# Opening, row factor and HGRN scores of a two-layer hybrid decoder trunk: two load queues, later squares, one compact score tile

## The chip, the cores and the metric

One core of one Trainium2 chip runs the whole program in one launch. The metric is the device time of one execution in microseconds (us); lower is better. The kernel before takes 960.01 us in the median of 3 executions (957.48 to 962.03).

## The reference, cut to what matters

Two layers, each a parallel mixer and a gated MLP, on x of 256 tokens by 1024 features, float32:

```python
for l in range(2):
    xn = rmsnorm(h, norm_mix_g[l])            # h * rsqrt(mean(h*h) + eps) * g
    z = xn @ w_in[l]                          # [RWKV-7 896 | attention 1152 | mLSTM 1032 | HGRN2 1024 | gates 4096]
    y = [rwkv7(zA), dilated_attention(zB), mlstm(zC), hgrn2(zD)]
    h = h + (sum(sigmoid(gate_b) * (y_b @ P_b) for b in 4)) @ w_out[l]
    xn = rmsnorm(h, norm_ffn_g[l])
    h = h + conv_ffn(xn)                      # up 1024 -> 2 x 2816, conv of width 3, silu gate, down
return rmsnorm(h, final_norm_g)

def hgrn2_chunk(q, k, v, logf):               # chunks of 64 tokens, 4 heads of 64 channels
    decay[t, s, c] = exp(b[t, c] - b[s, c])   # s <= t, b = cumsum(logf)
    attn[t, s] = sum_c q[t, c] * k[s, c] * decay[t, s, c]
    o = (q * exp(b)) @ S + attn @ v
```

The row factor of a norm, rsqrt(mean(h*h) + eps), is one number per token. It can therefore be applied to the columns of xn before a product, or to the product's result.

## The kernel before, in words

**Activations and weights.** The residual hT lies transposed in SBUF: 8 blocks of 128 features by 256 tokens. Every product with a weight is made in three matmuls (`mm3`, lines 343 to 345) of two-part numbers: hi times hi, lo times hi and hi times lo, where hi is the value rounded to fp32r and lo is the rest. Weights come as 314 tiles of up to 128x1024 in the order of `plan()`: DMA to `raw` (3 buffers), `hi` by a cast on ScalarE (ACT, line 298), `lo` by a subtraction on VectorE (DVE, line 299), 4 buffers each. A "column group" (`ct_group`) is 256 output features from two weight tiles: 2 x 8 x 3 = 48 matmuls of 128x256. `tok_group` gives tokens in the partitions.

**The norm.** `norm_block` makes X["u"] (xh, xl): h times g, without the row factor. `sum_block` squares the blocks and adds them up in `acc`, `row_factor` sums over features on TensorE (PE; psr) and takes the power -0.5 on GpSimd (POOL, `rc`), `row_bcast` spreads it by a matmul (psb) and an ACT copy to R. The first groups of a norm use X["u"] and are multiplied by R when they leave PSUM (`evac` for rw0 to rw3, line 591; `zf`, line 1393, for the up groups j < JU = 4). Meanwhile X["s"] (sh, sl), scaled by R, is made block by block: sh on ACT, sl on POOL (line 438). The groups that follow use it: HGRN's q and f (hgq, hgf), then hgt (v and g), and in the MLP up group 4.

**The opening.** SyncE's queue (SP) sends all loads: halves of weight tiles 0 and 1 between the quarters of x (hT), then the parameters pr, tile 2, rowt, lort, and at tile 3 the constants (ident, cft, cit). 16 warm-up matmuls run on PE. ACT works off xh, the squares and the casts in turn.

**Background work.** rwkv(), hgrn(), attn() and mlstm() are generators. `step()` advances them between matmuls of the column groups; the framework's scheduler then fixes each engine's order when the program is built, and each engine works strictly in that order.

**HGRN scores.** hgrn() has products of the forget gate in Pf (tile thf) and Q, doubles the segment length h from 1 to 128, and for each h makes scaled keys kt and queries qs (qsb, two buffers, line 1004 and 1007), a score product on PE (`pdl`) and a merge into the score tile A. A holds 8 blocks of 128x128; for h up to 32 the merge is four `copy_predicated` of 64x128 each (line 1069), for each token half pj and head parity par, since the two halves lie on A's two diagonal 64x64 blocks. The diagonal (`pdg`) is put in by four products with ident. For h = 64 and 128 ACT copies. Then `po` multiplies A with V.

Of the kernel before, what the change touches and what calls it, by code (L numbers as in the profile page):

```python
# [18 lines left out]
T = 256  # L19
# [10 lines left out]
WARM = 16  # L30
# [189 lines left out]
def trunk(tc, x, wst, prm, rows, lora, fing, cfd, cid, out, dbg=None, depth=DEPTH):  # L220
# [20 lines left out]
    nc.scalar.dma_start(pr0, prm[0][:, PC["gmix"][0]:PC["gmix"][0] + 8])  # L241
# [25 lines left out]
    dummy = cp.tile([128, 1], F32, name="dummy")  # L267
# [18 lines left out]
    def w_dma(i, part=None):  # L286
# [3 lines left out]
        nc.sync.dma_start(raws[i][:, q], wst[i, :, q])  # L290

    def w_split(i, parts=1):
        r = raws.pop(i)
        hi = wp.tile([128, GW], F32R, name=f"hi{i}", tag="hi", bufs=4)
        lo = wp.tile([128, GW], F32R, name=f"lo{i}", tag="lo", bufs=4)
        for q in range(parts):
# [3 lines left out]
        his[i] = (hi, lo)  # L300
# [3 lines left out]
    def w_ahead(n):  # L304
        while ws["dma"] < min(n, NG):
            if ws["dma"] == 6:
                late_consts()
            w_dma(ws["dma"])
            ws["dma"] += 1
# [92 lines left out]
    def sum_block(m):  # L402
        if m < 2:
            ac.activation(acc[:, m, :], hT[:, m, :], AF.Square)
        else:
            sq = sqp.tile([128, T], F32, name="sq")
            ac.activation(sq, hT[:, m, :], AF.Square)
# [48 lines left out]
    w_dma(0, 0)  # L456
    x_dma(0)
    x_dma(1)
    w_dma(0, 1)
# [11 lines left out]
    norm_block(0, pr0[:, 0:1])  # L471
    w_split(0, 2)
    for m in range(1, 8):
        norm_block(m, pr0[:, m:m + 1])
    w_split(1, 2)
    ws["split"] = 2


    for l in range(depth):
        with ExitStack() as lx:  # L480
# [3 lines left out]
            (nc.sync if l == 0 else nc.gpsimd).dma_start(pr, prm[l])  # L484
            if l == 0:
                w_ahead(5)
# [5 lines left out]
            with ExitStack() as mxs:  # L492
# [4 lines left out]
                (nc.sync if l == 0 else nc.gpsimd).dma_start(rowt, rows[l])  # L497
                lort = mp("lort", bufs=1).tile([128, 256], F32, name="lort")
                (nc.sync if l == 0 else nc.gpsimd).dma_start(lort, lora[l])
# [12 lines left out]
                ve.tensor_scalar(hb_ng, P("hng", 0, 2), 0.5, None, op0=OP.mult)  # L512
                ve.tensor_scalar(hb_bg, P("bg", 0, 32), 0.5, None, op0=OP.mult)
                ve.tensor_scalar(hpar[:, 32:36], P("w0", 0, 4), 0.5, None, op0=OP.mult)
                ve.tensor_scalar(c_ka, P("ka", 0, 2), -1.0, 1.0, op0=OP.mult, op1=OP.add)
                ve.tensor_scalar(c_mu, P("mu", 0, 7), -1.0, 1.0, op0=OP.mult, op1=OP.add)
# [69 lines left out]
                def rw_cols():  # L586
                    nonlocal R

                    def evac(g, ps):
                        for cs_, p_ in ps:  # L590
                            ve.tensor_tensor(zr[:, 2 * g:2 * g + 2, 1:][:, cs_], p_, bc2(R, cs_.stop - cs_.start), op=OP.mult)

                    def scale(ms):
                        for m in ms:
                            if m % 2 == 0:
                                tmp = gtp.tile([128, 2, T], F32, name="xsc", tag="gt")
                            scaled_block(m, P("gmix", m), R, tmp[:, m % 2, :])

                    u = X["u"]
                    if l == 0:  # L600
                        for m in range(8):
                            sum_block(m)
                    ps0 = ct_group("rw0", outer=(l > 0), a=u)
                    rc = row_factor(f"m{l}")
# [11 lines left out]
                    evac(2, ct_group("rw2", a=u))  # L616
# [322 lines left out]
                def hgrn(zz, sp):  # L939
# [20 lines left out]
                    thf = sp.tile([128, 2, T], F32, name="thf")  # L960
# [6 lines left out]
                    Q = sp.tile([128, 2, T], F32, name="Q")  # L967
                    gp.memset(Q, 1.0)
                    yield
# [67 lines left out]
                    while h <= 128:  # L1037
# [27 lines left out]
                        if h <= 32:  # L1065
                            for pj in range(2):
                                r = slice(pj * 64, pj * 64 + 64)
                                for par in range(2):
                                    ve.copy_predicated(A8[r, par * 4:par * 4 + 4, r].rearrange("p e (s w h) -> p e s w h", w=2, h=h)[:, :, :, 1, :],
                                                       hgm(i)[r].rearrange("p (s h) -> p s h", h=h)[:, None].to_broadcast([64, 4, 32 // h, h]),  # L1070
                                                       pds[0][r, :, par, :].rearrange("p e (s h) -> p e s h", h=h))
# [230 lines left out]
                rw_cols()  # L1302
                grw = rwkv()
# [61 lines left out]
            with ExitStack() as fxs:  # L1365
# [7 lines left out]
                JU = 4  # L1373
# [145 lines left out]
```

## Time and profile before

| | us |
|---|---|
| median of 3 executions (957.48 to 962.03) | 960.01 |
| the profiled execution, its own time | 969.59 |
| its span, first to last instruction | 967.0 |
| PE busy in the span | 936.8 |
| VectorE busy | 741.9 |
| ScalarE busy | 560.9 |
| GpSimd busy | 231.8 |

PE is busy in 97% of the span, so the time is what PE has to do, plus its waits, plus the stretches in which its clock was granted at half. The profile gives the waits by the line that waited and the engine that ended the wait, and by window the busy time and the granted clock (1.00 is 2.4 GHz, 0.50 is 1.2 GHz). A layer is its mixer, then its MLP.

### The profile page before, as it was taken

What the parts mean: (1) busy time and instruction counts of PE and PEld (TensorE: products, weight loads), DVE (VectorE), ACT (ScalarE), POOL (GpSimd) and SP (SyncE); (2) the same over time, 40 slices, a digit from 0 to 9 for tenths busy, and PEclk for the clock granted to TensorE, in tenths of its full rate; (3) what the DMA queues carried; (4) which work ended last, traced back from release to release, by engine and by line L of the source; (5) the groups of instructions that cost most, each with busy time, mean ns of one, the idle gap of its engine ahead of it and who ended that gap; (6) DMA issues with size and microseconds to landing.
All of it is one profiled execution on the core that took longest, in us unless ns stands there. A gap on an engine that the chain in (4) does not pass through costs nothing. (4 is left out here: it accounts for less than half of the span.)

```text
span 967.0 us, 21817 instructions
## 1 busy us (share of the span) xinstructions
PE 936.8 (97%) x8884; PEld 882.9 (91%) x8884; DVE 741.9 (77%) x1180; ACT 560.9 (58%) x953; POOL 231.8 (24%) x228
## 2 busy tenths in 40 slices
PE   7999999999999999999999999999999999999996
PEld 5988998989999999999998989888989999999885
DVE  6899775669688998876688996745878889888643
ACT  6874455565556676664478634454745657766533
POOL 3500220114308621120142004101223473111102
PEclk8999999999999999999999999999999999999998
DMA  7644353434466465556555344453445646656551
GB/s 251 197 152 145 109 165 119 148 121 161 142 197 196 153 211 183 196 172 195 186 179 177 124 128 144 133 150 123 149 137 186 202 142 215 204 192 192 186 194 66
DMA packets 48980, 160.09 MB, mean 166 GB/s; under 512 B 5872, under 2 KB 7408, under 8 KB 48752
## 3 DMA queue, kind: packets, MB, share of 16 engines
q1 hardware_dynamic: 46944, 155.55, 49.7%
q10 hardware_dynamic: 1584, 2.10, 0.8%
q8 instruction: 69, 1.13, 0.5%
q0 software_dynamic: 352, 1.06, 0.4%
q14 instruction: 31, 0.25, 0.1%
HBM read 156.06 MB, written 1.05 MB: 162 GB/s over the span
## 5 line engine op out<-in xcount | busy, mean ns | idle before, releaser
L299 DVE TENSOR_TENSOR lo<-raw,hi 128x1024 fp32r<-128x1024 f32 (+4 forms) x314 | 379.2, 1212 | 150.7 <-ACT hi L298 149.5
L298 ACT CAST hi<-raw 128x1024 fp32r<-128x1024 f32 (+4 forms) x314 | 308.1, 984 | 292.8 <-PE gate L344 77.5
L344 PE MATMUL up<-sl,hi 128*128 128x256 f32 x576 | 161.7, 281 | 3.3 <-POOL sl L438 3.1
L345 PE MATMUL up<-sh,lo 128*128 128x256 f32 x576 | 161.3, 280 | 0.0
L343 PE MATMUL up<-sh,hi 128*128 128x256 f32 x576 | 161.2, 280 | 0.0
L343 PE MATMUL gate<-sh,hi 128*128 128x256 f32 x512 | 146.8, 287 | 0.0
L345 PE MATMUL gate<-sh,lo 128*128 128x256 f32 x512 | 144.6, 282 | 0.0
L344 PE MATMUL gate<-sl,hi 128*128 128x256 f32 x512 | 143.1, 279 | 0.0
L344 PEld LDWEIGHTS up<-sl,hi 128*128 128x128 f32 x576 | 108.9, 189 | 4.3 <-POOL sl L438 4.3
L343 PEld LDWEIGHTS up<-sh,hi 128*128 128x128 f32 x576 | 110.0, 191 | 0.0
L345 PEld LDWEIGHTS up<-sh,lo 128*128 128x128 f32 x576 | 108.8, 189 | 0.0
L343 PEld LDWEIGHTS gate<-sh,hi 128*128 128x128 f32 x512 | 96.8, 189 | 3.8 <-issue 0.8
L345 PEld LDWEIGHTS gate<-sh,lo 128*128 128x128 f32 x512 | 96.9, 189 | 1.8 <-issue 0.8
L344 PEld LDWEIGHTS gate<-sl,hi 128*128 128x128 f32 x512 | 96.9, 189 | 0.6 <-issue 0.3
L1421 POOL TENSOR_TENSOR af<-sf,cvf 128x256 f32<-128x256 f32 x44 | 42.8, 974 | 165.2 <-ACT sf L1419 165.2
L1417 DVE SCALAR_TENSOR_TENSOR cvf<-up,pr,cvf 128x255 f32<-128x255 f32 (+1 forms) x144 | 68.9, 479 | 2.6
L553 POOL TENSOR_TENSOR merged<-merged,gt 128x512 f32<-128x512 f32 x16 | 34.4, 2152 | 88.8 <-DVE gt L551 86.2
L344 PE MATMUL dn<-alo,hi 128*128 128x256 f32 x176 | 49.4, 281 | 0.0
L345 PE MATMUL dn<-ahi,lo 128*128 128x256 f32 x176 | 49.4, 281 | 0.0
L343 PE MATMUL dn<-ahi,hi 128*128 128x256 f32 x176 | 49.3, 281 | 0.0
L1414 ACT ACTIVATE cvf<-up,pr 128x256 f32<-128x256 f32 x72 | 40.3, 560 | 1.6 <-DVE cvf L1417 1.6
L438 POOL TENSOR_TENSOR sl<-xsc,sh 128x256 fp32r<-128x256 f32 x32 | 39.2, 1258 | 0.0
(458 smaller groups left out, 2334.1 us busy)
## 6 DMA issues: line engine op xcount, KB each, us to landing
raw<-in_wst_dram SPq DMA_DIRECT2D x254, 512.0 KB, 3.8
raw<-in_wst_dram SPq DMA_DIRECT2D x28, 256.0 KB, 2.9
raw<-in_wst_dram SPq DMA_DIRECT2D x16, 448.0 KB, 3.1
raw<-in_wst_dram SPq DMA_DIRECT2D x8, 392.0 KB, 3.6
zrot<-zrot ACTq DMA_DIRECT2D x24, 64.0 KB, 3.0
cft<-in_cf_dram SPq DMA_DIRECT2D x1, 1041.0 KB, 6.6
hT<-in_x_dram SPq DMA_DIRECT2D x4, 256.0 KB, 6.1
raw<-in_wst_dram SPq DMA_DIRECT2D x8, 128.0 KB, 2.3
```

The costliest lines, as they stand in the source:

```text
L298: ac.copy(hi[:, c], r[:, c])
L299: ve.tensor_tensor(lo[:, c], r[:, c], hi[:, c].bitcast(F32), op=OP.subtract)
L343: te.matmul(o, lh, rh, start=first, stop=False)
L344: te.matmul(o, lh, rl, start=False, stop=False)
L345: te.matmul(o, ll, rh, start=False, stop=last)
L438: gp.tensor_tensor(lo[:, m, :], tmp, h[:, m, :].bitcast(F32), op=OP.subtract)
L553: gp.tensor_tensor(mo, mo, g, op=OP.add)
L1414: ac.activation(cv[:, n, :], z[:, n, :], AF.Identity, bias=P("fcb", cj), scale=P("fcw", 88 + cj))
L1417: ve.scalar_tensor_tensor(cv[:, n, d:], z[:, n, 0:T - d], P("fcw", 44 * i + cj), cv[:, n, d:], op0=OP.mult, op1=OP.add)
L1421: gp.tensor_tensor(a_, s, cv[:, 0, :], op=OP.mult)
```

## The change

- **Opening.** Tile 0 is sent by ACT's queue and the quarters of x by SP's, behind pr0. Tile 0 is split in quarters between the norm blocks. ident, pr, rowt, lort, cit and cft go between later tiles. 12 warm-up matmuls instead of 16. In layer 0 the squares wait on purpose (their scale `late1` is a one that is computed from the end of tile 1's hi) and stand behind rw0; the row factor is taken after rw1, and R in the middle of rw2, so that rw0, rw1 and rw2 are all in PSUM before R.
- **Row factor at evacuation.** hgq (both layers) and hgf (layer 0) use X["u"] and are multiplied by R on DVE; before, both used X["s"] and were copied by ACT. JU is 5 instead of 4.
- **HGRN scores.** Scores of both token halves stand in one compact tile Ad of 128 partitions by 4x2x64. The merge for h up to 32 is one `copy_predicated` of 128x256, the diagonal two products with idm (made on POOL). A takes the memory of Pf and Q (one tile PQ), so at h = 64 POOL clears its lower left part and ACT copies Ad onto its diagonal, after the last use of Pf and Q.

```diff
-    nc.scalar.dma_start(pr0, prm[0][:, PC["gmix"][0]:PC["gmix"][0] + 8])
+    between = {4: [lambda: nc.sync.dma_start(ident_t, cfd[:, 0:128])],
+               8: [lambda: nc.sync.dma_start(cit, cid)],
+               9: [lambda: nc.sync.dma_start(cft, cfd[:, 128:])]}
...
-    w_dma(0, 0)
+    nc.sync.dma_start(pr0, prm[0][:, PC["gmix"][0]:PC["gmix"][0] + 8])
+    w_dma(0, 0, nc.scalar)
     x_dma(0)
     x_dma(1)
-    w_dma(0, 1)
+    w_dma(0, 1, nc.scalar)
...
-    norm_block(0, pr0[:, 0:1])
-    w_split(0, 2)
-    for m in range(1, 8):
-        norm_block(m, pr0[:, m:m + 1])
+    norms((0, 1))
+    w_split(0, 4, (0, 1))
+    norms((2, 3, 4, 5))
+    w_split(0, 4, (2, 3))
+    norms((6, 7))
     w_split(1, 2)
+    ve.tensor_tensor(late1, his[1][0][:, GW - 1:GW].bitcast(F32), his[1][0][:, GW - 1:GW].bitcast(F32), op=OP.is_equal)
...
-                    ps1 = ct_group("rw1", a=u, mid=get_R)
+                    if l:
+                        get_rc()
+                        ps1 = ct_group("rw1", a=u, mid=get_R)
+                        ps2 = None
+                    else:
+                        ps1 = ct_group("rw1", a=u, mid=lambda: [sum_block(m, late1) for m in range(8)])
+                        get_rc()
+                        ps2 = ct_group("rw2", a=u, mid=get_R)
...
-                        ps = ct_group("hg" + nm)[0][1]
+                        direct = l == 0 or i == 0
+                        ps = ct_group("hg" + nm, **({"a": X["u"]} if direct else {}))[0][1]
-                        ac.copy(z, ps)
+                        if direct:
+                            ve.tensor_tensor(z, ps, bc2(R, 2), op=OP.mult)
+                        else:
+                            ac.copy(z, ps)
...
-                        for pj in range(2):
-                            r = slice(pj * 64, pj * 64 + 64)
-                            ve.tensor_tensor(A8[r, par * 4:par * 4 + 4, r], pds[par][r], ident[r, r][:, None, :].to_broadcast([64, 4, 64]), op=OP.mult)
+                        ve.tensor_tensor(Ad[:, :, par, :], pds[par], idm[:, None, :].to_broadcast([128, 4, 64]), op=OP.mult)
...
+                        if h == 64:
+                            gp.memset(A8[64:128, :, 0:64], 0.0)
+                            for pj in range(2):
+                                r = slice(pj * 64, pj * 64 + 64)
+                                ac.copy(A8[r].rearrange("p (a e) t -> p e a t", a=2)[:, :, :, r], Ad[r])
-                        if h <= 32:
-                            for pj in range(2):
-                                r = slice(pj * 64, pj * 64 + 64)
-                                for par in range(2):
-                                    ve.copy_predicated(A8[r, par * 4:par * 4 + 4, r].rearrange("p e (s w h) -> p e s w h", w=2, h=h)[:, :, :, 1, :],
+                        if h <= 32:
+                            ve.copy_predicated(Ad.rearrange("p e a t -> p (e a) t").rearrange("p e (s w h) -> p e s w h", w=2, h=h)[:, :, :, 1, :],
...
-                JU = 4
+                JU = 5
```

**What moves.** First ACT's order from tile 3's cast (raw_153 before, raw_190 after) and what stands around it in the opening; sq are the squares, lw the low-rank weights' two parts, hi tile casts, hpar a small parameter. Before:

```order
L298 CAST hi_224<-raw_151 128x1024
L407 ACTIVATE sq<-hT 128x256
L946 ACTIVATE hpar<-hpar 128x4
L407 ACTIVATE sq<-hT 128x256
L642 CAST lw<-lort 32x256 x4
L642 CAST lw<-lort 64x256 x2
L298 CAST hi_228<-raw_153 128x1024
L298 CAST hi_262<-raw_155 128x1024
L429 COPY Rm_330<-psbm_327 128x256
```

And after, from tile 2's cast (raw_188) to tile 5's (raw_195):

```order
L299 CAST hi_197<-raw_188 128x1024
L404 ACTIVATE acc<-hT,dummy 128x256 x2
L407 ACTIVATE sq<-hT,dummy 128x256 x2
L970 ACTIVATE hpar<-hpar 128x4
L299 CAST hi_201<-raw_190 128x1024
L407 ACTIVATE sq<-hT,dummy 128x256
L662 CAST lw<-lort 32x256 x4
L662 CAST lw<-lort 64x256 x2
L407 ACTIVATE sq<-hT,dummy 128x256 x3
L299 CAST hi_232<-raw_193 128x1024
L299 CAST hi_265<-raw_195 128x1024
```

All eight squares now stand between tile 2's and tile 4's cast, with the six lw casts ahead of the last three; before, six of them stood ahead of tile 2's. Tile 4 is the first of rw2.

Second, DVE in layer 0's HGRN stage, around one level of the doubling. Before, the level h = 16:

```order
L767 TENSOR_TENSOR LR<-pl,cft 128x512 x2
L1015 TENSOR_TENSOR Q<-Q,thf 128x8x32
L1069 COPY_PREDICATED A<-cit,pdl 64x4x2x16 x4
L792 COPY_PREDICATED TT<-cit,LR 32x256 x4
L1016 TENSOR_TENSOR thf<-thf 128x8x32
L998 TENSOR_TENSOR thq<-zhf,Q 128x4x64
```

After, the merges of h = 1 and 2, from the queries (qsb) of h = 4 to those of h = 8:

```order
L1034 TENSOR_TENSOR qsb_900<-zhq,PQ 64x8x32 x2
L1045 TENSOR_TENSOR PQ<-PQ 128x64x4
L1100 COPY_PREDICATED Ad<-cit,pdl 128x256
L300 TENSOR_TENSOR lo_1032<-raw_881,hi_1031 128x1024
L1046 TENSOR_TENSOR PQ<-PQ 128x64x4
L1028 TENSOR_TENSOR kt_840<-zhf,PQ 128x32x8
L1100 COPY_PREDICATED Ad<-cit,pdl 128x128x2
L1034 TENSOR_TENSOR qsb_901<-zhq,PQ 64x8x32 x2
```

The merge is one instruction per level. PE's order moves with it: before, 159 matmuls of column groups stand between the score products of h = 4 and h = 128 in layer 0, after 92; and the first `po` stands behind 584 of these matmuls of the layer before, behind 511 after. In layer 1 the score products of h = 4 to 128 span 166 before and 92 to 98 after.

## Rows read from the trace of the kernel before

**Rows 1.** The page: span, and each engine's busy us, share, instructions.
```profile
span 967.0 us, 21817 instructions
PE 936.8 (97%) x8884; PEld 882.9 (91%) x8884; DVE 741.9 (77%) x1180; ACT 560.9 (58%) x953; POOL 231.8 (24%) x228
```
**Rows 2.** PE's waits over the whole span: total us, times, longest.
```profile
PE up L344 <- POOL sl L438: 3.1, 3, 1.7
PE pdl L1045 <- DVE qsb L1004: 3.0, 3, 1.9
...
PE hgq L344 <- POOL sl L438: 2.3, 3, 1.0
...
PE psbm L426 <- POOL rcm L419: 1.6, 1, 1.6
```
**Rows 3.** Windows, layer 0: us; PE, PEld, DVE, ACT, POOL busy; PEclk, DMA share, GB/s.
```profile
6.40:13.02 6.62, 3.93 (x24) 3.08 (x23) 5.46 (x15) 6.58 (x17) 3.01 (x4) 0.91 1.05 394
13.02:18.65 5.63, 5.63 (x26) 5.63 (x27) 5.45 (x17) 4.60 (x11) 0.29 (x1) 0.50 0.97 360
...
24.01:48.62 24.61, 23.32 (x198) 22.84 (x199) 21.93 (x28) 20.16 (x39) 14.26 (x12) 1.00 0.61 196
...
84.31:86.92 2.61, 0.68 (x16) 0.48 (x16) 2.51 (x8) 1.78 (x3) 0.00 (x0) 1.00 0.54 185
86.92:90.33 3.41, 3.41 (x24) 3.29 (x21) 3.38 (x7) 0.00 (x0) 0.00 (x0) 0.50 0.41 153
90.33:110.00 19.67, 19.43 (x216) 18.29 (x215) 18.79 (x41) 8.68 (x15) 0.73 (x1) 1.00 0.42 126
```
**Rows 4.** ACT in the opening, in order of time: start, us, what [idle before].
```profile
3.84 0.62 ACT L298 CAST hi<-raw 128x512 fp32r<-128x512 f32 x1 [1.17 <-DMA raw<-in_wst_dram]
5.25 0.91 ACT L399 ACTIVATE xh<-hT,pr 128x256 fp32r<-128x256 f32 x2 [0.79 <-DMA hT<-in_x_dram]
...
12.40 1.03 ACT L298 CAST hi<-raw 128x1024 fp32r<-128x1024 f32 x1
...
14.05 0.40 ACT L407 ACTIVATE sq<-hT 128x256 f32<-128x256 f32 x1
14.36 2.51 ACT L642 CAST lw<-lort 32x256 fp32r<-32x256 f32 x6
```
**Rows 5.** DVE from 48.62 to 110 us by shape: count, busy us, mean ns.
```profile
L299 DVE TENSOR_TENSOR lo<-raw,hi 128x1024 fp32r<-128x1024 f32 x16 | 19.5, 1221 | 0.5 <-ACT hi L298 0.5
L1069 DVE COPY_PREDICATED A<-cit,pdl 64x128 f32<-64x128 int32 x24 | 7.0, 352 | 0.3
...
L1033 DVE TENSOR_TENSOR A<-pdg,ident_t 64x256 f32<-64x256 f32 x4 | 1.7, 420 | 0.1
```
**Rows 6.** DVE from 110 to 128 us: another merge from PSUM.
```profile
L809 DVE COPY_PREDICATED T__1430<-cit,pd 128x256 f32<-128x256 int32 x2 | 0.9, 452 | 1.1 <-PE pd L808 1.1
```
**Rows 7.** ACT from 100 to 112 us: copies from PSUM.
```profile
L775 ACT COPY bkT<-pb 128x512 f32<-128x512 f32 x2 | 1.1, 594 | 0.0
...
L1075 ACT COPY A<-pdl 64x256 f32<-64x256 f32 x2 | 0.6, 367 | 0.6 <-PE pdl L1056 0.6
```
**Rows 8.** Windows of both MLPs' starts and of layer 1's mixer, columns as in rows 3.
```profile
307.00:328.00 21.00, 19.80 (x164) 19.18 (x164) 17.36 (x21) 11.61 (x23) 18.84 (x18) 1.00 0.52 169
...
487.80:522.50 34.70, 33.34 (x279) 32.65 (x278) 29.70 (x57) 28.14 (x53) 16.55 (x18) 1.00 0.54 181
...
549.00:580.00 31.00, 29.09 (x307) 27.05 (x307) 30.30 (x68) 13.49 (x23) 0.86 (x2) 1.00 0.38 120
...
796.00:800.30 4.30, 2.21 (x17) 1.81 (x16) 3.25 (x4) 0.97 (x3) 4.30 (x4) 1.00 0.77 243
800.30:803.72 3.42, 3.42 (x18) 3.42 (x18) 3.42 (x6) 3.42 (x7) 1.83 (x3) 0.50 0.72 183
```
**Rows 9.** Windows of PE alone in both MLPs: us, busy, matmuls, clock, DMA.
```profile
340.00:424.00 84.00, 84.00 (x716) 1.00 0.60 193
...
830.00:897.00 67.00, 67.00 (x594) 1.00 0.60 193
```

More of the change, by code (lines that the diff above doesn't have):

```diff
@@ L266, in trunk @@
     ve.memset(ones, 1.0)
-    dummy = cp.tile([128, 1], F32, name="dummy")
+    dummy_t = cp.tile([128, 2], F32, name="dummy")
+    dummy, late1 = dummy_t[:, 0:1], dummy_t[:, 1:2]
     nhalf = cp.tile([128, 8], F32, name="nhalf")
@@ L284, in trunk, with w_dma @@
     raws, his = {}, {}
-    def w_dma(i, part=None):
+    def w_dma(i, part=None, eng=nc.sync):
         if not part:
@@ L289, in w_dma, with w_split @@
         q = slice(0, sizes[i]) if part is None else slice(sizes[i] // 2 * part, sizes[i] // 2 * (part + 1))
[L290 to L296, printed above, removed]
+        eng.dma_start(raws[i][:, q], wst[i, :, q])
+    def w_split(i, parts=1, some=None):
+        r = raws[i]
+        if i not in his:
+            his[i] = (wp.tile([128, GW], F32R, name=f"hi{i}", tag="hi", bufs=4),
+                      wp.tile([128, GW], F32R, name=f"lo{i}", tag="lo", bufs=4))
+        hi, lo = his[i]
+        for q in some or range(parts):
             c = slice(sizes[i] * q // parts, sizes[i] * (q + 1) // parts)
@@ L305, in w_ahead @@
         while ws["dma"] < min(n, NG):
-            if ws["dma"] == 6:
-                late_consts()
+            for send in between.pop(ws["dma"], ()):
+                send()
             w_dma(ws["dma"])
@@ L400, in norm_block, with sum_block @@
         ve.scalar_tensor_tensor(lo[:, m, :], hT[:, m, :], gcol, h[:, m, :].bitcast(F32), op0=OP.mult, op1=OP.subtract)
-    def sum_block(m):
+    def sum_block(m, one=1.0):
         if m < 2:
-            ac.activation(acc[:, m, :], hT[:, m, :], AF.Square)
+            ac.activation(acc[:, m, :], hT[:, m, :], AF.Square, scale=one)
         else:
             sq = sqp.tile([128, T], F32, name="sq")
-            ac.activation(sq, hT[:, m, :], AF.Square)
+            ac.activation(sq, hT[:, m, :], AF.Square, scale=one)
             (ve if m >= 6 else gp).tensor_tensor(acc[:, m % 2, :], acc[:, m % 2, :], sq, op=OP.add)
@@ L496, in trunk @@
                 rowt = mp("rowt", bufs=1).tile([128, 512], F32, name="rowt")
-                (nc.sync if l == 0 else nc.gpsimd).dma_start(rowt, rows[l])
                 lort = mp("lort", bufs=1).tile([128, 256], F32, name="lort")
-                (nc.sync if l == 0 else nc.gpsimd).dma_start(lort, lora[l])
+                if l:
+                    nc.gpsimd.dma_start(rowt, rows[l])
+                    nc.gpsimd.dma_start(lort, lora[l])
+                else:
+                    between[7] = [lambda: nc.sync.dma_start(rowt, rows[0]), lambda: nc.sync.dma_start(lort, lora[0])]
                 hpar = mp("hpar", bufs=1).tile([128, 66], F32, name="hpar")
@@ L596, in scale, with get_rc @@
                                 tmp = gtp.tile([128, 2, T], F32, name="xsc", tag="gt")
-                            scaled_block(m, P("gmix", m), R, tmp[:, m % 2, :])
+                            scaled_block(m, P("gmix", m) if l else pr0[:, m:m + 1], R, tmp[:, m % 2, :])
                     u = X["u"]
-                    if l == 0:
-                        for m in range(8):
-                            sum_block(m)
                     ps0 = ct_group("rw0", outer=(l > 0), a=u)
-                    rc = row_factor(f"m{l}")
+                    rc = None
+                    def get_rc():
+                        nonlocal rc
+                        rc = row_factor(f"m{l}")
                     def get_R():
@@ L615, in rw_cols @@
                     scale(range(4, 8))
-                    evac(2, ct_group("rw2", a=u))
+                    evac(2, ps2 or ct_group("rw2", a=u))
                     hi, lo = w_next()
@@ L959, in hgrn @@
                     ve.tensor_scalar(lbnH, lbA, -0.5, None, op0=OP.mult)
-                    thf = sp.tile([128, 2, T], F32, name="thf")
+                    PQ = sp.tile([128, 2, 2, T], F32, name="PQ")
+                    thf = PQ[:, 0]
                     thq = sp.tile([128, 2, T], F32, name="thq")
@@ L966, in hgrn @@
                     gp.memset(kt1, 0.0)
-                    Q = sp.tile([128, 2, T], F32, name="Q")
+                    Q = PQ[:, 1]
                     gp.memset(Q, 1.0)
+                    idm = sp.tile([128, 64], F32, name="idm")
+                    lm2 = C("lmask")
+                    gp.tensor_tensor(idm, lm2[:, 64:128], lm2[:, 0:64], op=OP.subtract)
                     yield
```

39 lines of the change are left out of this document (20 added, 19 removed).

## The prediction

> **What bounds the kernel now.** The page's head comes first: PE is busy for 936.8 of 967.0 us [rows 1]. The change takes away none of PE's weight products, so it can gain only what PE waits, what it does at half clock, and the four warm-up matmuls. The table of PE's waits names the places [rows 2]: MLP groups that wait for POOL's sl (3.1 us), HGRN's score products that wait for the queries on DVE (3.0), hgq that waits for sl (2.3), and the spread of the row factor that waits for POOL (1.6). Then the windows show what such a wait costs beyond itself. In layer 0's opening PE is busy for 3.93 of 6.62 us, and the next 5.63 us are granted at 0.50: 26 matmuls take 0.217 each there, against 0.113 at full clock (67.0 us for 594) [rows 3, 9]. The same happens after the score wait at 84.31 (next 3.41 us at 0.50) [rows 3] and in layer 1's MLP (busy 2.21 of 4.30 us, next 3.42 us at 0.50) [rows 8]. So the clock fell to 1.2 GHz behind each of these waits, and such a wait is paid about twice. I make the sum against the profiled execution, 969.6 us, and carry the difference to the median, 960.0.
>
> **Opening (term 1).** DMA share is 1.05 at 394 GB/s from 6.40 to 13.02 us [rows 3], with one queue. I therefore let the second queue bring nothing: the two halves of tile 0 and the four quarters of x, 1.5 MB, land as now, only in another order. Were the second queue's rate added on top, tile 0's 0.5 MB would cost x nothing, 1.3 us at that rate, and the first matmuls would end by so much sooner. The Trainium skill (page "DMA: Bandwidth & Descriptors", section "Issuing engines are not separate DMA queues") speaks against that: transfers that several engines issue run on the same 16 DMA engines and interleave, and only issue time is saved. By this rule the split's own share is 0, as in my sum; the busy share above agrees.
>
> What gains is the order on ACT and DVE. The first data came at 3.84 (tile 0) and 5.25 (x) [rows 4]; sharing the engines, I let both be there at 5.2. ACT then does two quarter casts (0.35 each, estimated from half casts of 0.62), two xh (0.91), the early xsc (0.45, as an xh), two quarter casts, six xh (0.45 each): 10.7 [rows 4]. DVE's xl is 0.42 behind (its price for 256 columns [rows 5]), so weight tile 0's 24 matmuls end at 11.5. Tile 1's two casts end at 11.9, its lo parts (about 0.65 each, half of a whole tile's 1.22) let the next 24 matmuls run from 12.1 to 14.8, at full clock. Before, these 48 ended at 18.65, the end of the half-clock window. Tile 2: cast 1.03, lo 1.22 [rows 4, 5], the lo behind six small operations on pr, for which I allow 0.9: 14.7, no wait; its 24 matmuls end at 17.5, against 18.65 + 24 x 0.117 = 21.5 before. That is 4 us.
>
> Then ACT falls behind. From 12.9 it has four squares (1.6), the small exponential that sits behind DVE's lo (to 15.1), tile 3's cast (1.03), a square, the six lw casts (2.51), three squares (1.2) and only then tile 4's cast: 21.2, its lo at 22.4 [rows 4]. PE is through rw1 (24 more matmuls) at 20.2, so it waits 2.2 us in front of rw2: the new wait in the place of the 1.6 for the row factor and of hgq's share. The other 168 matmuls up to hgt are 19.0 us, the small products of the norm and of the low-rank part 1.6, and I allow 1.0 for the latter, whose inputs now come from a DVE that has the hgq evacuation (about 0.6, as ACT's copy of that size [rows 7]) on top: 22.4 + 19.0 + 1.6 + 1.0 = 44.0. Before, hgt begins at 48.62, the end of a window [rows 3]. **Gain 4.6.** Bounds: 7.8 if both new waits are hidden; 2.0 if the half clock comes as before (26 matmuls x 0.104 = 2.7).
>
> **HGRN scores (term 2).** Layer 0: 24 merges, 7.0 us busy, become 6 of 0.45 (nearest row: a 128x256 merge from PSUM, 452 ns [rows 6]), and four diagonal products of 0.42 become two: 5.2 us less on DVE, which is busy 18.79 of 19.67 us from 90.33 to 110 [rows 3, 5]. PE's loss there is 2.61 - 0.68 = 1.9, plus 1.7 for the half clock, plus 19.67 - 19.43 = 0.2 from 90.33 on: 3.8 [rows 3], the most that can come back. But PE's order is tightened too: between the scores of h = 4 and h = 128 stand 92 matmuls instead of 159. PE needs 92 x 0.113 + 2.5 for score products + 1.8 for pl + some 2 for changes between them, 16.7. DVE has in that stretch five lo (1.2 each), some 16 products (0.34 each where they overlap, an estimate from 0.42), three pairs of queries (0.85), six merges and two score masks (0.6), 17.9 [rows 5, 6]. So PE waits about 1.0 again. At the end a chain is added: POOL clears (I allow 0.2 past the copies' own wait), ACT copies Ad to A twice (0.59 each) and the h = 64 scores twice (0.37 [rows 7]), 2.1 us, in front of `po`, behind which PE stands after some 10 matmuls (1.1): another 1.0. **Gain 3.8 - 2.0 = 1.8**, bounds 3.8 and -1.5 (the half clock comes again, at either place). Layer 1: PE waits 1.9 in 549 to 580 [rows 8]. There only 6 matmuls stand between the last scores and `po`, so the copy chain shows 1.4, the DVE 0.5 to 1: **gain 0**, bounds 1.9 and -2.
>
> **hgq on X["u"], layer 1 (term 3).** From 487.8 to 522.5 PE loses 1.36 us [rows 8], nearly all hgq's wait for sl. hgf is 48 matmuls, 5.5 us, later, when sl is there. The evacuation moves from ACT to DVE, which is busy 29.7 of 34.7 us there; it stays hidden while the lo tiles are ahead. **Gain 1.3**, bounds 1.4 and 0.
>
> **JU = 5 (term 4).** Layer 0: 21.0 - 19.8 = 1.2 us of wait; layer 1: 4.30 - 2.21 = 2.1, and 1.7 of the 3.42 at half clock [rows 8]. Group 5 starts 5.5 us after group 4, and POOL is through before. Cost: one more evacuation per layer, about 0.6 on DVE, which is busy 17.36 of 21.0 us in layer 0's start; the tiles of hi and lo that stand ready (4 buffers) hide it, and without them it would stand on the path. **Gain 1.2 + 3.8 = 5.0**, bounds 5.0 and 2.5.
>
> **Sum:** 4.6 + 1.8 + 0 + 1.3 + 5.0 = 12.7. Profiled 969.6 becomes 956.9, the median 960.0 becomes 947.3; I say **947**. Bounds of all terms: 940 and 959.
>
> **Rivals.**
> (a) All waits go and none come: 7.8 + 3.8 + 1.9 + 1.4 + 5.0 = 19.9, so 940. For it: DVE loses 10 us of work in two layers. Against: ACT's order above, in which nothing is shorter, and the tightened PE order.
> (b) The opening's clock still falls: by the sum above PE idles some 1.5 us between the first and the second quarter of x, and 4 fewer warm-up matmuls precede it. Term 1 is 2.0, the time 950. For it: the drop before came with 3.93 of 6.62 us busy. Against: slower matmuls fill the 2.2 us that PE would otherwise wait for tile 4.
> (c) The scores are placed too early: DVE falls behind at each level, the clock falls in both layers. Terms 2 are -1.5 and -2: 953. It decides where a wait in front of pdl or po becomes as long as the 1.9 us at 84.31.
> (d) Slower: the pace of PE's products. With the same code, clock and tile sizes the up groups take 84.0/716 = 0.117 us per matmul in layer 0 and 67.0/594 = 0.113 in layer 1 [rows 9]. 314 tiles make up to 7500 such matmuls, 30 us between all at the one and all at the other pace, and layer 0's 1056 up matmuls are at the slow one. If shifted waits put 5000 more there, 20 us are lost and the time is 967. It decides from about 3200 on, where the 12.7 are used up. For it: the pace is set by something other than clock or shape. Against: nothing in the change aims at it, and it can as well go to the fast side, 937.
> (e) The edits do not reach the path, since waits return elsewhere (the merge into `wo`, the MLP's lo tiles): within 0.5%, some 957.
>
> **How the numbers follow.** 0.5% of 960 is 4.8 us, about what a measurement of this kernel can tell from no change. Forecast (943 to 951) 0.55; (a) with the fast side of (d) 0.13; (b) 0.12; (c) 0.09; (e) 0.06; (d) slow 0.05. The range 937 to 956 takes in (a), (b) and (c) and leaves out half of (e), (d) and the lower end, under 2 in 10. Faster by over 0.5% (below 955.2): 0.55 + 0.13 + 0.12 + 0.07 = 0.87. Same: 0.02 + 0.06 + 0.01 = 0.09. Slower: 0.04.
>
> **What would show it.** Opening: hgt's first matmul near 44 us, no half-clock window before 20 us, a PE wait of about 2 us in front of rw2 behind ACT's hi or DVE's acc and lo. HGRN: six merges per layer near 0.45 us, DVE still over 90% busy, short waits of pdl and one of po for ACT's copies, full clock at 80 to 95 us. hgq and up without waits for sl; no half clock in layer 1's MLP. The prediction would be wrong if the waits for pdl and po grow past 4 us, if a half-clock window returns in three places, or if the share of slow-paced matmuls changes by thousands.

## The result

The changed kernel takes 957.07 us (median of 20 runs, 952.51 to 963.77), the kernel before 962.40 beside it (20 runs, 957.48 to 969.83): a ratio of 0.9935, interval 0.991 to 0.996. It is faster, by 5.3 us in the medians and 6.3 by the ratio where 12.7 were forecast, and it lies 1.1 us above the range. The forecast started from 960.01, the median of three executions; 20 of them give 962.40, so 2.4 us of the miss against 947 are in that start, and the rest is in the gain.

The two profiled executions differ by more (969.59 and 956.87, spans 967.0 and 955.1), by chance exactly the 12.7 of the forecast. Nearly half of that isn't the change, which only the runs below show. Each of PE's products runs at one of two paces, and in the profile of before the slow one held through most of layer 0's up and down products, in that of after it did not: some 1,170 slow products fewer, 5.3 us at 4.5 ns each. The page of after, against [rows 1]:

```profile
span 955.1 us, 21775 instructions
PE 929.6 (97%) x8880; PEld 876.0 (92%) x8880; DVE 730.2 (76%) x1148; ACT 564.3 (59%) x956; POOL 237.6 (25%) x230
```

PE's waits from 6 to 955 us of after, against [rows 2] (total us, times, longest):

```profile
PE rw L343 <- DVE zr L602: 3.7, 2, 1.9
PE pp L343 <- ACT yhC L584: 2.7, 2, 1.4
PE pdl L1073 <- DVE Ad L1061: 2.3, 1, 2.3
PE psrm L416 <- DVE acc L410: 1.3, 1, 1.3
PE psw L691 <- DVE la L663: 1.1, 1, 1.1
PE psrf L416 <- DVE acc L410: 1.1, 1, 1.1
PE pdl L1073 <- DVE qsb L1034: 0.8, 2, 0.4
PE pdl L1087 <- DVE qsb L1037: 0.6, 1, 0.6
```

The waits for POOL's sl are gone, as the change intends, and so is POOL's rcm in layer 0 (the row factor's input, 1.6 us before). New ones stand in their place: rw3 in both layers for zr, the evacuation of the first group (1.7 and 1.9), psrm for the sum of squares, psw for la. pdl still waits: 3.7 in all, against 3.9 before (3.0 of it in [rows 2], the rest in two smaller rows).

The opening of after by windows, columns as in [rows 3]:

```profile
6.83:20.32 13.49, 12.82 (x96) 11.90 (x96) 12.51 (x36) 12.30 (x29) 4.09 (x6) 1.00 1.01 397
20.32:23.73 3.41, 1.73 (x13) 1.46 (x13) 3.03 (x6) 3.28 (x4) 0.99 (x2) 1.00 0.04 14
23.73:27.14 3.41, 3.41 (x19) 3.41 (x18) 1.57 (x2) 0.45 (x1) 1.00 (x1) 0.50 0.87 245
27.14:35.75 8.61, 6.87 (x59) 6.66 (x59) 6.45 (x8) 6.20 (x14) 4.91 (x6) 1.00 0.61 209
35.75:47.95 12.20, 11.09 (x98) 10.93 (x97) 12.01 (x17) 10.24 (x21) 7.58 (x7) 1.00 0.39 130
```

Up to 20.3 us the forecast holds to 0.2 us: 96 products in place of the half-clock window of before. Then three things come in a row. PE stands; the DMA share is 0.04, so nothing is being loaded either; and the clock falls to 0.50 behind PE's wait (1.2 GHz, as in [rows 3]). Why the loads stop is read from the queue of SP (12 to 36 us) and from ACT, both of after:

```profile
SPq L289 <- DVE lo L300: 10.3, 6, 2.9
SPq L289 <- DVE rcm L418: 4.6, 1, 4.6
```
```profile
20.67 2.92 ACT L299 CAST hi<-raw 128x1024 fp32r<-128x1024 f32 x3
26.69 1.04 ACT L299 CAST hi<-raw 128x1024 fp32r<-128x1024 f32 x1 [3.09 <-DMA raw<-in_wst_dram]
29.45 1.05 ACT L299 CAST hi<-raw 128x1024 fp32r<-128x1024 f32 x1 [1.72 <-DMA raw<-in_wst_dram]
30.40 0.36 ACT L429 COPY Rm<-psbm 128x256 f32<-128x256 f32 x1
```

There are three raw buffers (the tiles that loads land in), and DVE's lo gives each free. The lo of the tile that ACT reached late (behind the squares and the lw casts) holds SP 4.6 us (the row names rcm, which stands on DVE right behind that lo), so no weight load is issued from 17.5 to 23.0 us. ACT then waits 3.09 and 1.72 us for raw tiles. The copy of the row factor, Rm, stands in ACT's order behind the second of these casts and ends at 30.8; DVE's zr needs Rm, rw3 needs the PSUM that zr frees, and PE waits 1.7 us more. hgt's first product starts at 47.95, against 48.62 [rows 3].

### The profile page after: what moved, and what is told of

Same layout as the page of the kernel before. It is cut to its first block, busy times and chain, and to the rows that moved or that the text cites. A ratio compares the mean times of both kernels' runs of the same rounds, so it can differ in the third digit from the quotient of the medians.

```text
span 955.1 us, 21775 instructions
## 1 busy us (share of the span) xinstructions
PE 929.6 (97%) x8880; PEld 876.0 (92%) x8880; DVE 730.2 (76%) x1148; ACT 564.3 (59%) x956; POOL 237.6 (25%) x230
## 4 chain that ended last, share of the span: by engine, by line
PE 77%; DVE 8%; POOL 4%; ACT 4%; issue 3%; DMA 3%; POOLq 0%; SPq 0%; ACTq 0%; DVEq 0%
PE up L345 6%; PE up L343 6%; PE up L344 6%; PE gate L343 6%; PE gate L345 6%; PE gate L344 5%; PE dn L343 4%; PE dn L345 4%; PE dn L344 4%; DVE lo L300 3%; POOL sl L438 2%; POOL xsc L1430 2%; DMA raw<-in_wst_dram 1%; PE pp L343 1%; ACT hi L299 1%
## 5 line engine op out<-in xcount | busy, mean ns | idle before, releaser
L345 PE MATMUL up<-sh,lo 128*128 128x256 f32 x544 | 150.8, 277 | 0.5 <-DVE lo L300 0.4
L343 PE MATMUL up<-sh,hi 128*128 128x256 f32 x544 | 150.6, 277 | 0.0
L344 PE MATMUL up<-sl,hi 128*128 128x256 f32 x544 | 150.4, 276 | 0.0
L345 PEld LDWEIGHTS up<-sh,lo 128*128 128x128 f32 x544 | 102.2, 188 | 1.3 <-DVE lo L300 1.3
L344 PEld LDWEIGHTS up<-sl,hi 128*128 128x128 f32 x544 | 102.2, 188 | 0.0
L343 PEld LDWEIGHTS up<-sh,hi 128*128 128x128 f32 x544 | 102.1, 188 | 0.0
L1451 DVE SCALAR_TENSOR_TENSOR cvf<-up,pr,cvf 128x255 f32<-128x255 f32 (+1 forms) x136 | 65.1, 479 | 2.4
L344 PE MATMUL up<-xl,hi 128*128 128x256 f32 x160 | 45.7, 287 | 0.0
L345 PE MATMUL up<-xh,lo 128*128 128x256 f32 x160 | 45.3, 284 | 0.0
```

What stands on the lines that cost most here:

```text
L343: te.matmul(o, lh, rh, start=first, stop=False)
L344: te.matmul(o, lh, rl, start=False, stop=False)
L345: te.matmul(o, ll, rh, start=False, stop=last)
L1451: ve.scalar_tensor_tensor(cv[:, n, d:], z[:, n, 0:T - d], P("fcw", 44 * i + cj), cv[:, n, d:], op0=OP.mult, op1=OP.add)
```

## The experiments

The table has, for each kernel, the median with its number of runs, the ratio to the kernel before (run on the same chip) with its interval, and four marks of its profile: where hgt and where ml of layer 0 start, and in layer 1 the stretches from rw to hgt, from hgt to ml, and from up to down. "S+J" is the compact scores and JU = 5.

| kernel | edits in it | us (n) | ratio | hgt 0 | ml 0 | rw-hgt 1 | hgt-ml 1 | up-dn 1 |
|---|---|---|---|---|---|---|---|---|
| before | none | 962.4 (20) | 1 | 48.62 | 175.91 | 34.66 | 128.19 | 127.39 |
| after | all | 957.07 (20) | 0.9935 [0.991, 0.996] | 47.95 | 176.32 | 35.13 | 125.69 | 124.57 |
| e1 | without the opening | 954.96 (10) | 0.990 [0.9868, 0.9932] | 47.63 | 176.56 | 31.82 | 127.85 | 124.83 |
| e2 | without compact scores | 960.03 (10) | 0.9986 [0.9962, 1.001] | 47.11 | 177.94 | 32.75 | 128.49 | 124.83 |
| e3 | without JU = 5 | 962.64 (10) | 0.9999 [0.9966, 1.0032] | 47.91 | 175.49 | 31.82 | 126.87 | 130.19 |
| e4 | without direct hgq/hgf | 954.16 (5) | 0.9929 [0.9897, 0.996] | 51.24 | 175.66 | 34.01 | 125.53 | 124.87 |
| e5 | S+J alone | 954.33 (7) | 0.9908 [0.9867, 0.995] | 47.73 | 173.32 | 34.17 | 125.61 | 124.83 |
| e6 | all, lw held back | 957.67 (10) | 0.9932 [0.9899, 0.9966] | 41.82 | 175.83 | 32.35 | 127.22 | 124.26 |
| e7 | all, hgq/hgf over POOL | 956.15 (10) | 0.991 [0.9883, 0.9937] | 47.20 | 176.38 | 35.90 | 125.55 | 126.18 |
| e8 | all, ten small pairs more | 965.56 (10) | 1.0008 [0.9979, 1.0036] | 47.58 | 176.03 | 35.10 | 125.63 | 129.79 |
| e9 | S+J, one pair per layer | 955.46 (9) | 0.9915 [0.9889, 0.9942] | 48.82 | 174.39 | 35.67 | 125.30 | 125.67 |
| e10 | S+J, lw held back | 953.93 (7) | 0.9917 [0.9884, 0.995] | 49.11 | 174.62 | 32.10 | 126.71 | 124.29 |
| e11 | S+J, opening, lw held back | 952.45 (4) | 0.9896 [0.9843, 0.9949] | 43.31 | 172.57 | 32.21 | 126.61 | 124.95 |
| e12 | e11, direct hgq in layer 1 | 952.96 (6) | 0.9893 [0.9864, 0.9922] | 44.12 | 173.27 | 32.28 | 127.72 | 124.79 |

The intervals are 5 to 10 us wide, so two kernels are told apart by their times only where they differ by several us. The marks are finer, but each comes from one profile: a half-clock window in a stretch loses 1.7 us of its 3.41, and 200 products more at the slow pace cost 0.9. In e6, e11 and e12 hgt starts before 26 products that stand ahead of it in the other kernels, 22 of hgf's 48 weight products and four of the low-rank part, some 3.0 us; their first mark is to be read with that added.

**e1 to e4: each part undone.** e1 takes the opening of before; e2 the four diagonal products and the 24 merges; the other two are one line each:

```diff
-                JU = 5
+                JU = 4
```
```diff
-                        direct = l == 0 or i == 0
+                        direct = False
```

> The changed kernel with the opening of before (one queue, squares and parameters at the old place, 16 warm-ups, rw2 behind the evacuations); the other three edits stay. The forecast's theory: the new opening is worth 4.6 us, so hgt starts at 48.6 instead of 44.0, and the time is 4.6 us above the changed kernel's. Rival, from the two traces: the new opening gains only 0.7 us up to hgt (48.62 against 47.95), because a half-clock window and a wait for the row factor's evacuation came in; then hgt starts near 48.6 again, and the time is at most 1 us above the changed kernel's.

> The changed kernel with the old HGRN scores (four diagonal products, 24 merges in halves, A in its own tile). The forecast's theory: layer 0 loses 1.8 us between hgt and the merge product ml, layer 1 nothing, so the time rises 1.8. Rival, from the traces: the compact tile lost 1.1 us in layer 0 (128.4 against 127.3 from hgt to ml) and gained 2.5 in layer 1 (125.7 against 128.2), so undoing it gives 127.3 and 128.2 and raises the time by 1.4. Third: those two differences are where the stretches happen to lie to the loads, and not the scores; then both stretches stay within 0.5 us of the changed kernel's.

> The changed kernel with JU = 4. The forecast's theory: 5.0 us slower, 1.2 in layer 0's and 3.8 in layer 1's MLP, with a half-clock window back in layer 1's. Rival: 2.8 us slower, in layer 1 alone, since layer 0's MLP of the changed kernel has a half-clock window of its own (303.6 us) and waits there for the row factor and not for sl.

> The changed kernel with hgq (and in layer 0 hgf) on the scaled x again, in both layers, as before. The forecast's theory: layer 1 loses 1.3 us to hgq's wait for sl, layer 0 about 1.3 too (hgq's wait of 38.3 us comes back), 2.6 together. Rival, from the traces: 1.9 in layer 1 (11.80 to 13.71 from hgq to hgt); in layer 0 the scaled x is now later than before, so hgq waits longer than the 1.3 us of before and the time rises by 4 or more.

Measured by the medians: 2.1 us faster without the opening, 3.0 slower without the compact scores, 5.6 slower with JU = 4, 2.9 faster without the direct hgq/hgf. By the ratios, each to the kernel before on its own chip, it is 3.4 faster, 4.9 slower, 6.2 slower and 0.6 faster. The intervals of e2 and e3 lie apart from that of the changed kernel, those of e1 and e4 overlap with it. So the scores and JU = 5 carry the gain; the opening and the direct hgq/hgf bring nothing that shows, and whether they cost something is not shown by these two times. e1's rival expected "at most 1 us above" and missed the sign too; e4's rival expected 4 us or more of loss, because hgt does start 3.3 us later (51.24), and missed that ml does not (175.66 against 176.32).

That JU = 4 brings the waits back is seen in e3's two MLP starts (296 to 330, 770 to 830 us), and the half clock that sets in towards the end of the longest:

```profile
PE up L344 <- POOL sl L438: 1.4, 2, 1.0
PE psrf L416 <- DVE acc L410: 1.1, 1, 1.1
...
PE up L344 <- POOL sl L438: 2.2, 2, 1.7
```
```profile
790.49:793.90 3.41, 2.99 (x14) 2.99 (x15) 3.25 (x7) 3.41 (x8) 2.53 (x4) 0.50 0.62 201
```

In e2 pdl waits 5.9 us in layer 0 alone (47 to 178 us), against the 3.9 of before in both layers:

```profile
PE pdl L1069 <- DVE qsb L1028: 2.9, 4, 1.9
PE pdl L1069 <- DVE A L1057: 2.5, 1, 2.5
PE pdl L1080 <- DVE qsb L1031: 0.3, 1, 0.3
PE pdl L1083 <- DVE qsb L1031: 0.2, 1, 0.2
```

**e5: scores and JU = 5 alone**, the kernel before with e1's and e4's edits both undone.

> The kernel before with the compact HGRN scores and JU = 5 alone: opening and hgq/hgf as before. The forecast's theory: opening and direct hgq are worth 4.6 + 1.3 us, so this is 5.9 us slower than the changed kernel, about 963. Rival, from the runs that undid one part each (undoing the opening gave -2, undoing the direct hgq -3): up to ml in layer 0 DVE sets the end, what PE gains in front of hgt it waits again for pdl, and the two edits cost more than they bring; then this kernel is at or below the changed one's 957, 952 to 956, with ml's first product in layer 0 at 175 to 176.5 us as in every version.

Measured 954.33, against 957.07 with everything (0.9908 and 0.9935; the intervals overlap). The two edits that were left out were forecast to bring 5.9 us, and the medians have them cost 2.7. The rival's time is right; its ml, 175 to 176.5, is not: 173.32. The windows from the first product to hgt and from hgt to ml show it, in the order after, e4, e5:

```profile
6.83:47.95 41.12, 35.93 (x276) 34.37 (x277) 35.56 (x65) 32.47 (x66) 18.57 (x19) 0.96 0.65 234
47.95:176.32 128.37, 125.63 (x1638) 114.09 (x1637) 93.93 (x169) 68.31 (x122) 15.31 (x16) 1.00 0.44 140
```
```profile
6.97:51.24 44.27, 36.98 (x276) 34.67 (x277) 37.20 (x68) 34.84 (x70) 18.79 (x19) 0.96 0.60 217
51.24:175.66 124.42, 124.41 (x1638) 113.33 (x1636) 94.42 (x164) 66.77 (x120) 15.20 (x16) 1.00 0.43 144
```
```profile
7.21:47.73 40.52, 36.28 (x279) 35.26 (x277) 34.82 (x63) 31.36 (x64) 21.67 (x19) 0.92 0.68 234
47.73:173.32 125.59, 125.46 (x1639) 114.12 (x1637) 93.78 (x164) 67.28 (x121) 15.05 (x16) 1.00 0.42 142
```

PE is idle 5.2 us ahead of hgt and 2.7 behind it in after, 7.3 and 0.0 in e4, 4.2 and 0.1 in e5. With the direct hgq PE goes ahead without the scaled x, and meets DVE later: the diagonal product Ad, for which pdl waits, starts on DVE at nearly the same time with and without it, and 3 us sooner with the opening of before and no direct hgq. DVE is not late by its own work alone: in after it waits 1.3 us for ACT's nk ahead of Ad, in e4 and e5 0.6. DVE of after, e4 and e5:

```profile
76.00 0.75 DVE L1061 TENSOR_TENSOR Ad<-pdg,idm 128x256 f32<-128x256 f32 x2
```
```profile
75.66 0.76 DVE L1061 TENSOR_TENSOR Ad<-pdg,idm 128x256 f32<-128x256 f32 x2
```
```profile
72.83 0.75 DVE L1041 TENSOR_TENSOR Ad<-pdg,idm 128x256 f32<-128x256 f32 x2
```

**e6: lw out of the way.** The six casts take a scale that is 1.0 and made from R:

```diff
+                    lateR = rw.tile([128, 1], F32, name="lateR")
+                    ve.tensor_tensor(lateR, R[:, 0:1], R[:, 0:1], op=OP.is_equal)
+                    hw_ = lambda d, s_, p0, p1: ac.activation(d, s_, AF.Copy, scale=lateR[p0:p1, 0:1])
...
-                        hi_(lw[0:32, i], src)
+                        hw_(lw[0:32, i], src, r, r + 32)
```

> The changed kernel with the six lw casts (2.5 us on ACT) and the three subtractions on DVE held back until the row factor R is there. The forecast's theory: what is taken off the opening is gained; the wait for the evacuation in front of rw3 (2.0 us) goes, hgt starts 2 us earlier, and so does ml (174.3). Rival, DVE-bound to ml: hgt starts 2 us earlier, the pdl waits in HGRN grow by as much, and ml's first product stays at 175.5 to 176.5. Third: the casts come back in front of psw, where PE waits for la, and hgt itself does not move.

hgt starts 6.1 us sooner, at 41.82; 3.0 of that are the 26 products that now stand behind it. PE waits 1.6 us for POOL in front of psbm, as in the kernel before, but rw3 does not wait for zr, no half clock is granted before 113 us, ACT waits for no raw tile from 14 to 36 us, and pdl does not wait. Yet ml starts at 175.83 and the time is 957.67. The rival's sum is right and its place wrong: HGRN's output product pyD waits behind POOL, whose small power for the norm stands in this kernel behind attention's rotation, which waits for its transfer. The wait, and the windows of it and of the half clock behind it:

```profile
PE pyD L580 <- DVE PQ L1136: 2.5, 1, 2.5
```
```profile
111.20:113.40 2.20, 0.21 (x25) 0.10 (x11) 1.75 (x3) 0.00 (x0) 0.41 (x1) 1.00 0.25 62
113.40:120.22 6.82, 6.34 (x61) 5.95 (x62) 3.44 (x7) 1.79 (x3) 3.04 (x2) 0.50 0.37 118
```

**e7: less work on DVE.**

```diff
-                            ve.tensor_tensor(z, ps, bc2(R, 2), op=OP.mult)
+                            ac.copy(z, ps)
+                            gp.tensor_tensor(z, z, bc2(R, 2), op=OP.mult)
```

> The changed kernel with hgq's and hgf's row factor taken by an ACT copy and a POOL product in place of one DVE product from PSUM: about 1.2 us less on DVE in layer 0, 0.6 in layer 1. DVE-bound to ml: the pdl waits in layer 0 (2.6 and 0.7 us in the changed kernel) shrink by about 1.2 and ml starts that much sooner, 175.1. The forecast's theory (DVE hides the evacuation): nothing moves. Third: POOL's product delays zhq by 2 us and slows DVE beside it, pdl waits longer, ml later.

ml starts at 176.38, as in the changed kernel, and pdl waits 2.7 for Ad instead of 2.3. So 1.4 us less work on DVE did not bring Ad sooner (76.13 against 76.00). The edit does not decide why: the third reading holds too, since POOL's product takes 2.1 us and DVE's next step on zhq starts at 51.24 instead of 48.83. That the wait belongs to the order in which PE and DVE come to the scores is argued, not shown, and why ml starts at 175.5 to 177.9 in every kernel with the direct hgq in layer 0 and at 172.6 to 175.9 without it is not settled further.

**e8 and e9: the pace.** e8 puts in front of five up groups of each layer, e9 behind up1 of each layer:

```diff
+                        pk = pmm.tile([128, 512], F32, name="pkick", tag="mm")
+                        for h in range(2):
+                            te.matmul(pk[:, h:h + 1], acc[:, 0, h * 128:(h + 1) * 128], ones[:, 0:1], start=True, stop=True)
```

> The changed kernel with two tiny 128x1 products put in front of five up groups of each layer; nobody reads them. For the two paces of the weight products (113 and 118 ns at the same granted clock). If the pace is drawn anew at each interruption of the stream and then holds: no stretch at one pace crosses such a point unless by chance, slow stretches of over 200 products in a row become rare, and changes of pace stand right at the new products. If it is set by something slower (heat, traffic): a slow stretch runs on through them. The cost of the products themselves is about 10 x 0.2 = 2 us.

> The kernel of e5 (compact scores and JU = 5 alone) with one pair of tiny 128x1 products behind the second up group of each layer; nobody reads them. In the run with ten such pairs per two layers each pair that had weight products on both sides flipped their pace (113 to 118 ns or back), and in every profile the row factor's pair psbf leaves up at the slow pace for the next 188 products. If a pair flips the pace: the slow stretch behind psbf ends after some 24 products, up in layer 0 runs at 113 ns, and no execution carries 118 ns through the down products; the time is 1 to 2 us below e5's 954.3 (0.85 and, in 3 of 10 profiles, 6.7 us saved, against 0.7 for the pair) and spreads less. If the flips were chance: slow for 188 products or more as before, and the time is 1.4 above.

In e8 every one of the ten pairs changed the pace: from fast to slow, or from slow to fast. Windows of e8's up products between pairs at 344.1, 378.5, 395.3 and 412.7 us (us, PE busy and count, PEld, DVE, ACT, clock, DMA):

```profile
344.81:378.50 33.69, 33.69 (x288) 33.64 (x286) 12.66 (x27) 7.30 (x13) 1.00 0.62 214
379.10:395.20 16.10, 16.10 (x144) 16.10 (x143) 5.00 (x11) 3.36 (x6) 1.00 0.57 197
395.95:412.70 16.75, 16.75 (x144) 16.68 (x142) 5.24 (x12) 3.35 (x6) 1.00 0.55 189
413.30:420.00 6.70, 6.70 (x61) 6.70 (x61) 2.11 (x5) 1.50 (x3) 1.00 0.48 167
```

That is 0.117, 0.112, 0.116 and 0.110 us per product with the ends counted in, at granted clock 1.00 throughout; from start to start it is 0.1178 and 0.1133. In e9 both psbf turned the pace slow and both added pairs turned it back. e9's expectation had the slow 188 products behind psbf in every profile; they are there in 10 of the 14. The ten pairs cost 8.5 us, four times what was expected, and in e9 the pair's price (up to down in layer 0 takes 124.24, in e5 123.91) eats what it saves: 955.46 against 954.33, no gain. The runs of e9 spread over 3.5 us, those of e5 over 8.1.

**e10 to e12: is the opening of use once lw is away?** e10 is e5 with e6's edit, e11 is e4 with it, e12 has `direct = l == 1 and i == 0` as well.

> The kernel of e5 (opening and hgq/hgf as before) with the lw casts and subtractions held back until the row factor R is there, as in e6. Tells whether the gain in front of hgt in e6 (6 us) came from the new opening or from the lw work alone. If from lw alone: hgt starts at 43 to 45 us here too (47.7 in e5). If it takes both: hgt moves by less than 1 us, since here the squares and parameters stand first on ACT and DVE and PE waits for the row factor in front of psbm (1.9).

> The changed kernel with lw held back and hgq/hgf on the scaled x as before (e4 and e6 together). If the new opening can be of use once lw does not stand in ACT's and DVE's way: the wait in front of rw3 (3.4 us in e4) goes, hgt starts at 46 to 48 instead of 51.2, and ml in layer 0 at 173 or below, the time at or below 952. If what PE gains in front of hgt is waited again behind it whatever the order: ml at 175 to 176.5, the time as e4's 954 to 957.

> The kernel of e11 with hgq of layer 1 alone on the unscaled x, as in the changed kernel. The forecast's term (1.3 us for hgq's wait in layer 1): from rw to hgt in layer 1 30.9 or less, against 32.2 in e11, and the time 1.3 below e11's 952.5. Rival: what layer 1 gained in the profiles with the direct hgq (33.6 to 31.6, both without slow pace) is the same time that holding lw back gains (31.3 in e11 without the direct hgq), so the two do not add: 31.3 again without slow pace, and 952 to 953. Layer 0 as e11: ml at 172 to 173.

With the old opening lw held back gains nothing ahead of hgt (49.11). With the new one hgt moves from 51.24 (e4) to 43.31, 3.0 of it by order (46.3 without that, inside the expected 46 to 48), and ml from 175.66 to 172.57, the earliest of all; the time, 952.45, just misses the expected 952. e11's windows, PE idle 3.7 us ahead of hgt and not at all behind it:

```profile
7.16:43.31 36.15, 32.49 (x250) 31.06 (x251) 33.72 (x63) 30.03 (x61) 18.64 (x19) 0.95 0.67 241
43.31:172.57 129.26, 129.26 (x1664) 117.91 (x1663) 96.22 (x170) 72.06 (x129) 15.23 (x16) 1.00 0.43 145
```

Two rows of e11 tell what changed, ACT's wait in front of Rm (14 to 36 us) and SP's for raw buffers (12 to 36 us):

```profile
ACT Rm L429 <- PE psbm L426: 2.4, 1, 2.4
```
```profile
SPq L289 <- DVE lo L300: 19.2, 7, 6.4
```

The loads still stop, with none issued from 17.8 to 22.6 and from 23.7 to 30.5 us. But Rm now stands ahead of the casts that would wait for them: it starts at 23.91, as soon as psbm is done, and not at 30.40.

e11 and e12 have the lowest medians here, 952.45 and 952.96. e12's interval, 0.9864 to 0.9922, reaches just into that of the changed kernel, 0.991 to 0.996; the medians stand 4 us apart. From e1, e5 and e10 (ratios 0.990 to 0.992) they are not told apart. The direct hgq of layer 1 added nothing (32.28 against 32.21), as the rival had it.

## Why the prediction was wrong

**What bounds the kernel** was right: the gain is in PE's waits and half-clock windows. Which of the waits would not come back elsewhere was not.

**Term 1, the opening (4.6 forecast; 0.7 at hgt, nothing or a loss in the time).** The sum failed behind tile 4. Up to there it is right: no half clock before 20 us, rw1's last product at 20.4 (20.2 forecast), then PE waits 1.6 us (2.2 forecast; 1.3 in front of psrm and 0.3 for a lo), and psw waits 1.1 (1.0 allowed). But "the other 168 matmuls up to hgt are 19.0 us" let them run without a wait. I followed ACT's lateness to DVE's lo and to PE, and not to the raw buffer that the lo frees, to SP's next load, and back to ACT and Rm. That chain is rw3's 1.7 us, and the half clock behind the psrm wait is another 1.7. With 0.2 for rw1's later end and 0.1 for psw, less the 0.6 by which the first wait is shorter than forecast, they are 3.1 of the 3.9 between 44.0 and 47.95; the other 0.8 is not told apart. e6 and e11 show that the lw work, where it stands in this opening, costs rw3's wait: with lw held back the wait is gone, and hgt starts at 41.8 and 43.3, or 44.8 and 46.3 with the 26 products. They do not show that the raw buffers do: their loads stop as well, and what moved together with lw is Rm, ahead of the casts that wait. That link is read from the trace of after alone.

The step that the second queue brings no rate held: from 2 to 8 us, while ACT's queue and SP's both have loads under way (tile 0's last part landed at 6.57), after moves 265 GB/s at a DMA share of 0.92, and before with the weights and x on one queue 285 at 0.92. The rule that transfers issued by several engines share the 16 DMA engines (the Trainium skill, "DMA: Bandwidth & Descriptors", "Issuing engines are not separate DMA queues") agrees with this.

The second error is that the sum ends at hgt, and that hgq/hgf of layer 0 had no term of its own. It was inside term 1, as PE's wait for sl that goes. e4 against after shows that this time is waited again at pdl (PE idle behind hgt 2.7 us with the edit, 0.0 without, and ml 0.7 later with it): a wait that is removed ahead of a stretch in which PE waits for DVE is not a gain until that stretch is followed too.

**Term 2, the scores.** Layer 0's 1.8 is what they bring by themselves: from hgt to ml 125.59 in e5, against 127.29. In the changed kernel the other edits hide it (128.37, and 130.83 in e2 without the scores, so they bring 2.5 there). Layer 1's 0 was too low: 2.5 us (128.19 to 125.69; 128.49 again in e2). Its step "DVE 0.5 to 1, copies 1.4" put new waits as high as the old ones; pdl waits 1.0 there, and po for no copy. The merges cost a little more than the 0.45 forecast, DVE of after from 61 to 122 us:

```profile
L1100 DVE COPY_PREDICATED Ad<-cit,pdl 128x256 f32<-128x256 int32 x6 | 3.2, 530 | 0.0
```

**Term 3, hgq in layer 1 (1.3).** Its wait for sl is gone, but from rw to hgt the changed kernel's profile takes 35.13, against 34.66. There ACT waits for the low-rank weights:

```profile
487.98 1.25 ACT L662 CAST lw<-lort 32x256 fp32r<-32x256 f32 x3 [2.81 <-DMA lort<-in_lora_dram]
```

lort landed 5.5 us after its issue, 3.7 before, and what stands behind it, the row factor and zr, made PE wait 0.5 and 1.9. e7 and e8 show 35.1 to 35.9 too, with the same late lort (e7 with a half-clock window besides), e1, e2 and e3 31.8 to 32.8 with the same edit; without it e4 and e5 take 34.0 to 34.2. So in front of hgt the edit gains about 2 in some executions and loses about 1 in others. Why lort lands late in some was not found. With lw held back (e11) the 2 us are there without the edit. Read at ml, the sum of the table's two columns, little of it is left: 159.7 in e1 (with a half-clock window) and 158.7 in e3, against 159.5 and 159.8 in e4 and e5, and 160.8 in after.

**Term 4, JU = 5 (5.0).** Right: 5.6 us by e3; in layer 1 up to down 124.57, against 127.39 before and e3's 130.19, with the half clock gone. Why e3 is 2.8 above before there, with the same JU, is open. In layer 0 a half-clock window at 303.62 hid the gain in this one profile.

**The sum.** Terms 2 and 4 were forecast at 6.8 together and measured 8.9 in e5 (4.8 to 12.8 by its interval). Terms 1 and 3 were forecast at 5.9; e5 leaves no gain of theirs, and by the medians a cost of 2.7. Rival (e), "waits return elsewhere", gave the time of 957, with the wrong places. Rival (d) held what sets one execution apart from the next: its two paces are real; that tiny products flip them was not foreseen.

## What to carry to other kernels

When an engine is late, follow the buffer that it holds to the queue that refills it, and back to the engine, and look at what stands behind the next wait in its order: the second round (rw3, 1.7 us) cost as much here as the first. A wait removed in front of a stretch in which the engine waits for another is a gain only if that other comes sooner too; read the mark behind the stretch (here ml's first product), not the one in front, and count what stands ahead of a mark before comparing it. Undo each part of a change by itself: two of four edits carried the gain, and keeping them with the opening, once lw was out of its way, gave the lowest medians, if not by a margin that these runs can show.

## What the hardware showed

PE's 128x256 products run at 0.1133 or 0.1178 us from start to start, at granted clock 1.00 with the same operands. The pace mostly holds until the stream is interrupted; seven changes in the 14 profiles have no break beside them. The added pairs of tiny products flipped it in all 12 cases (ten in e8, two in e9), and psbf in 26 of its 28 (two a profile): in layer 0 of e5 and e12 the products are slow before it and behind it. Longer waits also changed it, not always. So an interruption by tiny products nearly always flips the pace, and is not shown to be what sets it. In 10 of the 14 profiles psbf leaves layer 0's up slow for exactly 188 products, until a wait for a lo; in before (after 130 products), e2, e6 and e10 it stayed or turned slow again behind such a wait, for 1297 to 1422 products, some 6 us. Down in layer 0 takes 62.07 us in before and 59.69 for all but one of its products in after:

```profile
425.61:487.68 62.07, 62.07 (x528) 62.07 (x528) 2.94 (x7) 1.00 0.59 191
```
```profile
421.51:481.20 59.69, 59.69 (x527) 59.69 (x528) 2.94 (x7) 1.00 0.61 197
```

What in the engine the two paces are was not found. Half-clock windows are as loose: the same opening had them at 23.73 (after), 10.15 (e2), 8.84 and 32.73 (e3) and 32.32 us (e4). One profile of such a kernel can be some 6 us off; the marks of several, with the windows at half clock and the slow stretches told apart, are finer.
